# A state-space loop: the in-turn products go to the end of a step, and the sum of GpSimd's stack becomes an adding DMA

## The chip, the cores and the metric

The kernel runs on one core of one Trainium2 chip. The metric is the device time of one execution in microseconds (us), here the median of several runs. The engines go by these names: PE is TensorE (matrix products), DVE is VectorE, ACT is ScalarE, POOL is GpSimd, SP is the engine that issues most DMAs. Each engine works through its own queue in order and waits on semaphores for the others.

## The reference

Two layers work on 1024 latent tokens and 256 context tokens of width 1024. Layer 0 mixes the tokens by a diagonal state-space model (S5) in both directions, then comes a gated feed-forward layer; layer 1 is attention with a feed-forward layer. Only the S5 mixer is touched here. Cut to what matters:

```python
def s5_direction(u, h0, ar, ai, bbr, bbi, C_re, C_im, reverse, want_y):
    ug = u.reshape(Bn, L, S5_G, S5_GC).swapaxes(0, 1)
    br = jnp.einsum('lbgc,gpc->lbgp', ug, bbr)
    bi = jnp.einsum('lbgc,gpc->lbgp', ug, bbi)
    ...
    _, _, hr, hi = lax.associative_scan(s5_combine, (a_r, a_i, br, bi), reverse=reverse, axis=0)
    ...
    y = (jnp.einsum('lbgp,gcp->blgc', hr, C_re.astype(jnp.float32))
         - jnp.einsum('lbgp,gcp->blgc', hi, C_im.astype(jnp.float32))).reshape(Bn, L, D)
```

There are 64 groups of 16 channels, 64 complex states for each group, and two directions.

## The kernel before

The token axis is cut into blocks of 8 tokens, so that one scan runs over 160 block states. Each complex state is turned by a table of cosines and sines, so that the scan itself is real: a turn in, a scan with a real decay, a turn back. Two groups in both directions make one step of a loop, 32 steps of work in all (n = 0 to 32, with a drain). The engines' queues in this loop hold exactly the order in which the code is written (the line with `pinned.update`). What a step n does, by the names in the code:

- `stack_in(n+4)` makes the input matrices of a later step: two products on GpSimd, `sb` and `su`, and their sum into `sb`. `stack_out(n+6)` makes output matrices in the same manner on VectorE, `sc` and `su`; their sum is an adding DMA, issued from GpSimd. Sums that are owed stand in the list `owed`, and `settle` issues them.
- `turned(n+3)` transposes `sb` on TensorE into PSUM, ScalarE copies it to `bt`, and small products of `sc` with `bb1` build a lag kernel in PSUM. In even steps `lag_out` takes that to the tile `kt`, by two copies on ScalarE and one instruction on VectorE; a DMA stores it, and `lag_in` loads it as `mt`.
- `in_products(n+2)` multiplies `bt` with the tokens `ug` into two PSUM tiles `psA`, of which there are two in all. `in_turn(n+2)` multiplies these with the tables `tcs` and `tsn` to `ww` and `pq` on VectorE, and an adding DMA from GpSimd sums them into `ww`.
- `scans(n)` runs six scans from `ww` into `zz`, with the decay `r8` in PSUM. `turn_back(n)` makes `qc` and `qs` from `zz`, and `out_products(n-1)` multiplies those of the step before, and `ug` with `mt`, into an output tile that `out_copy` takes away on ScalarE.
- `tables_a`, `tables_b`, `tables_c` make the tables of step n+3: a part on ScalarE (`ty`, `tn`), one instruction on VectorE (`ty` from `tn`), and the sines on ScalarE.
- Every fourth step `load_u` loads the next `ug` into one of two buffers and ScalarE copies one column of it.

VectorE's queue of one step was: scans, `ww`, `pq`, `qc`, `qs`, `ty`, in even steps `kt`, then `sc`, `su`. All profile rows bear line 198, that of the helper which records each instruction, so the tiles' names tell them apart.

Of the kernel before, what the change touches and what calls it, by code (L numbers as in the profile page):

```python
# [18 lines left out]
F32 = mybir.dt.float32  # L19
# [164 lines left out]
def trunk(tc, I, out, dbg=None):  # L184
# [20 lines left out]
    V, S, Q, T, D_ = (Engine(*e) for e in zip("VSQTD", (nc.vector, nc.scalar, nc.gpsimd, nc.tensor, nc.sync)))  # L205
    dma = D_.dma_start

    def mul(o, a, b, e=V):
        e.tensor_tensor(o, a, b, op=ALU.mult)

    def add(o, a, b, e=V):
        e.tensor_tensor(o, a, b, op=ALU.add)
# [10 lines left out]
    def gather(o, a):  # L223

        Q.dma_start(o, a, accum_op=ALU.add)
# [14 lines left out]
    def pool(name, bufs=1, side="left", space=None):  # L240
        kw = {} if space is None else {"space": space}
        cm = tc.tile_pool(name=name, bufs=bufs, side=side, reuse_waits="tile", **kw)
        p = cm.__enter__()
        opened.append((p, cm))
        return p
# [461 lines left out]
    def w_in_norm(p, xc):  # L707

        acc = p.tile([128, 640], F32, name="acc", tag="nacc", bufs=1)
        square(acc, xc[:, 0])  # L710
        for f in range(1, 8):
            sq = p.tile([128, 640], F32, name="sq", tag="ns", bufs=3)
            square(sq, xc[:, f])
            add(acc, acc, sq, (V, Q)[f % 2])
        yield
        r = rstd_of(acc, D, 640, 2, psA)
        for f in range(8):
            mul(xc[:, f], xc[:, f], r, (V, Q)[f % 2])
        yield
# [31 lines left out]
    g = w_in_norm(st, x)  # L751
# [9 lines left out]
    g = w_in_norm(st, x)  # L761
# [18 lines left out]
    ge = pool("ge", 1, "right")  # L780
# [3 lines left out]
    def load_c(q):  # L784
        c = ge.tile([128, 2, 8, C16], F32, name="cc", bufs=6)
        dma(c.rearrange("p a b c -> p a (b c)"), I["c12"][q])
        coef[q] = c

    def sign_c(q):
        c = coef[q]  # L790
        S.activation(c[:, 0], c[:, 0], AF.Copy, scale=sg[:, 1:2])

    sh = [128, 4, TB, C16]
    AHEAD = 6

    owed = []

    def settle():

        for o, a in owed:  # L800
            gather(o, a)
        owed.clear()

    def stack(k, name, p_, x1, x2, e, p, nb):

        k0 = 4 * k

        def pw(t):
            return t.rearrange("p t g -> p g t")[:, k0:k0 + 4, :, None].to_broadcast(sh)

        def cf(t):
            return t[:, :, None, :].to_broadcast(sh)

        u = ge.tile(sh, F32, name="su", tag="su" + name, bufs=1 if e is Q else 2)
        a = p.tile(sh, F32, name=name, tag=name, bufs=nb)
        mul(a, pw(p_[0]), cf(x1), e)
        mul(u, pw(p_[1]), cf(x2), e)
        if e is Q:
            add(a, a, u, e)
        else:  # L820
            owed.append((a.rearrange("p g t c -> p (g t c)"), u.rearrange("p g t c -> p (g t c)")))
        return a.rearrange("p g t c -> p g (t c)")

    def stack_in(k):

        k0 = 4 * k
        sbs[k] = stack(k, "sb", bp, bb1[:, k0:k0 + 4], bb2[:, k0:k0 + 4], Q, ge, 2)
# [6 lines left out]
    def swap(k):  # L834

        cs = scs[k][0]
        cw = gp.tile([128, 4, 128], F32, name="cw", bufs=4)
        dma(cw[0:64], cs[64:128])
        dma(cw[64:128], cs[0:64])
        cws[k] = cw  # L840
# [40 lines left out]
    def lag_in(q):  # L881
        mt = gp.tile([128, 4, 128], F32, name="mt", bufs=3)
        for t in range(TB):
            dma(mt[16 * t:16 * t + 16],
                ktd[q][:, 0:16, 16 * (7 - t):16 * (7 - t) + 128].rearrange("g c k -> c g k"))
        mts[q] = mt

    def load_u(ft):
        ug = gp.tile([128, 8, JX], F32, name="ug")
        dma(ug[:, :, :J], ubd[ft].rearrange("t c g j -> (t c) g j"))  # L890
        copy(ug[:, :, J:JX], ug[:, :, 0:1])
        return ug
# [11 lines left out]
    def turns_in(t):  # L904

        return pairs(t)
# [4 lines left out]
    def tables_a(n):  # L911

        def flat(t):
            return t[:, :2 * sht[2]].rearrange("p (a b) -> p a b", a=2)[:, :, :2 * JX]

        ty = flat(wp.tile([128, 1024], F32, name="ty", tag="wr"))
        tn = flat(wp.tile([128, 1024], F32, name="tn", tag="wb", bufs=6))
        for i in range(4):
            l = slice((i % 2) * JX, (i % 2) * JX + JX)
            S.activation(ty[:, i // 2, l], idx[:, l], AF.Copy, scale=f8[:, 4 * n + i:4 * n + i + 1])  # L920
        S.activation(tn, ty, AF.Identity, bias=magic)
        tys[n] = ty, tn
# [50 lines left out]
    def in_products(n):  # L973

        bt, ug = bts.pop(n), ugs[n // 4]
        va = []
        for sw in range(2):
            v = psA()
            for i in range(4):
                d = i % 2  # L980
                T.matmul(v[:, i // 2, d * J:d * J + J], bt[:, i, 64 * sw:64 * sw + 128],
                         ug[:, (2 * n + i // 2) % 8, d:d + J], start=True, stop=True)
            va.append(v)
        return va

    def in_turn(n, va):

        pq = []
        for v, t, nm in zip(va, tab[n], ("ww", "pq")):
            p_ = gt.tile(sh4, F32, name=nm, tag=nm, bufs=NW if nm == "ww" else NPC)  # L990
            mul(p_.rearrange("p (g d) j -> p g d j", g=2),
                v[:, :, :2 * J].rearrange("p g (d j) -> p g d j", d=2), turns_in(t))
            pq.append(p_)
        owed.append(tuple(p_.rearrange("p a j -> p (a j)") for p_ in pq))
        return pq[0]

    def states(w):
        z = wp.tile([128, 1024], F32, name="zz", tag="wb", bufs=6)[:, :4 * J].rearrange("p (a b) -> p a b", a=4)
        Q.memset(z[:, 0::2, 0:1], 0.0)
        Q.memset(z[:, 1::2, JC - 1:JC], 0.0)  # L1000
        return w, z

    def scans(n, w, z):

        def scan(o, x_, i, init):
            m_ = o.shape[-1]
            V.tensor_tensor_scan(o, r8[:, 4 * n + i:4 * n + i + 1].to_broadcast([128, m_]), x_,
                                 init, op0=ALU.mult, op1=ALU.add)

        for i in (1, 3):  # L1010
            scan(z[:, i, 0:JC - 1][:, ::-1], w[:, i, 0:JC - 1][:, ::-1], i, 0.0)
        for i in (0, 2):
            scan(z[:, i, 1:J], w[:, i, 0:J - 1], i, 0.0)
        for i in (1, 3):
            scan(z[:, i, JC:J][:, ::-1], w[:, i, JC:J][:, ::-1], i, z[:, i, 0:1])
# [35 lines left out]
    NS5 = 32  # L1051
    pend = {}
# [5 lines left out]
    for n in range(NS5 + 1):  # L1058
        if n % 4 == 0 and n + 4 < NS5:
            ugs[n // 4 + 1] = load_u(n // 4 + 1)  # L1060
        if n % 2 == 0 and (n + AHEAD + 2) // 2 < NS5 // 2:
            load_c((n + AHEAD + 2) // 2)
        if n + 2 < NS5:
            swap(n + 2)
        if n % 2 == 1 and (n + 1) // 2 < NS5 // 2:
            lag_in((n + 1) // 2)
        if n + 4 < NS5:
            stack_in(n + 4)
        settle()
        if n + 2 < NS5:  # L1070
            va = in_products(n + 2)
        if n < NS5:
            scans(n, *pend[n])
        if n + 3 < NS5:
            tables_a(n + 3)
        if n > 0:
            py = out_products(n - 1, rot)
        if n + 2 < NS5:
            pend[n + 2] = states(in_turn(n + 2, va))
            settle()  # L1080
        if n > 0:
            out_copy(n - 1, py)
        if n < NS5:
            rot = turn_back(n, pend.pop(n)[1])
        if n + 3 < NS5:
            tables_b(n + 3)
        if n + 3 < NS5:
            turned(n + 3)
            if n % 2 == 0:
                lag_out((n + 2) // 2)  # L1090
        if n + AHEAD < NS5:
            stack_out(n + AHEAD)
        if n % 2 == 1 and (n + AHEAD + 1) // 2 < NS5 // 2:
            sign_c((n + AHEAD + 1) // 2)
        if n + 3 < NS5:
            tables_c(n + 3)
        if n % 4 == 1 and n > 1:
            store_y(n // 4 - 1)
        if n == 28:
            ws = Weights([((I[a][i],), 8) for _ in range(2) for a, i in  # L1100
                          [("swg", i) for m in range(8) for i in (8 + m, m)] + [("swo", m) for m in range(8)]], 4, 2)
            ws.load()
        if n == 31:
            ws.ahead = 0
            ws.ahead = 0
            first_w = [ws.whole(8)]
# [43 lines left out]
    def tB():  # L1150
        return hB.tile([128, 2, 640], F32R, name="hb", tag="hb")
# [37 lines left out]
    for c in range(2):  # L1189
        av = []  # L1190
        for m in range(8):
# [10 lines left out]
            o = tB()  # L1202
# [610 lines left out]
    pend = []  # L1813
# [108 lines left out]
```

## Time and profile before

| | |
|---|---|
| time, median of 3 runs | 3428.85 us (3422.14 to 3429.99) |
| time of the profiled execution | 3414.58 us |
| its span, first to last instruction | 3412.8 us |
| TensorE (PE) busy | 3179.5 us, 93% |
| VectorE (DVE) busy | 2784.1 us, 82% |
| ScalarE (ACT) busy | 1745.9 us, 51% |
| GpSimd (POOL) busy | 1052.3 us, 31% |
| mean granted TensorE clock | 0.980 of full speed |

The shares are means over stages with different limits. The loop that is changed lies between about 204 us and 485 us of the span. Clock 1.00 is 2.4 GHz, 0.50 is 1.2 GHz. A row of the timeline gives the start, the duration, the engine, the operation with its written and read tiles, and in brackets how long the engine was idle before it and what ended that.

### The profile page before, as it was taken

What the parts mean: (1) busy time and instruction counts of PE and PEld (TensorE: products, weight loads), DVE (VectorE), ACT (ScalarE), POOL (GpSimd) and SP (SyncE); (2) the same over time, 40 slices, a digit from 0 to 9 for tenths busy, and PEclk for the clock granted to TensorE, in tenths of its full rate; (3) what the DMA queues carried; (4) which work ended last, traced back from release to release, by engine and by line L of the source; (5) the groups of instructions that cost most, each with busy time, mean ns of one, the idle gap of its engine ahead of it and who ended that gap; (6) DMA issues with size and microseconds to landing.
All of it is one profiled execution on the core that took longest, in us unless ns stands there. A gap on an engine that the chain in (4) does not pass through costs nothing. (4 is left out here: it accounts for less than half of the span.)

```text
span 3412.8 us, 55310 instructions
## 1 busy us (share of the span) xinstructions
PE 3179.5 (93%) x20468; PEld 2922.0 (86%) x20468; DVE 2784.1 (82%) x4640; ACT 1745.9 (51%) x3234; POOL 1052.3 (31%) x812
## 2 busy tenths in 40 slices
PE   5887789999999999999999989989989899999999
PEld 3877779999999999999988767767777799889998
DVE  5979977878888989888866678888886788898887
ACT  4456662425333444344555557777775544454443
POOL 2356620101112121121234345555554411221111
PEclk7989989999999999999999999999999999999999
DMA  6457776552333323322335742222225333233232
GB/s 231 131 128 157 154 184 212 207 184 88 106 108 101 120 87 112 114 72 83 123 118 159 198 138 76 81 74 75 72 72 162 126 103 105 90 124 105 97 109 75
DMA packets 191775, 414.69 MB, mean 122 GB/s; under 512 B 22224, under 2 KB 73360, under 8 KB 190480
## 3 DMA queue, kind: packets, MB, share of 16 engines
q1 hardware_dynamic: 182288, 392.27, 36.0%
q0 software_dynamic: 9216, 18.88, 3.1%
q8 instruction: 162, 2.65, 0.3%
q14 instruction: 109, 0.89, 0.1%
HBM read 326.89 MB, written 53.49 MB: 111 GB/s over the span
## 5 line engine op out<-in xcount | busy, mean ns | idle before, releaser
L198 PE MATMUL psB<-hs,wb 128*128 128x320 f32 (+1 forms) x7392 | 1002.2, 297 | 24.4 <-DVE wb L198 16.9
L198 PEld LDWEIGHTS psB<-hs,wb 128*128 128x128 f32 x7392 | 991.1, 189 | 34.3 <-DVE wb L198 22.1
L198 ACT ACTIVATE wb<-wr 128x512 fp32r<-128x512 f32 (+3 forms) x704 | 404.7, 593 | 431.2 <-PE psB L198 219.6
L198 DVE TENSOR_TENSOR wb<-wr,wb 128x512 fp32r<-128x512 f32 (+3 forms) x704 | 492.3, 709 | 160.4 <-ACT wb L198 159.5
L198 PE MATMUL psB<-hb,wb 128*128 128x320 f32 (+1 forms) x3360 | 601.4, 340 | 10.5 <-ACT hb L198 4.7
L198 PEld LDWEIGHTS psB<-hb,wb 128*128 128x128 f32 x3360 | 544.8, 188 | 62.9 <-ACT hb L198 5.9
L198 POOL TENSOR_TENSOR ws<-wr 128x512 f32<-128x512 f32 x176 | 243.6, 1389 | 1151.1 <-DMA wr<-in_fi 535.4
L198 ACT ACTIVATE wb<-ws 128x512 fp32r<-128x512 f32 x352 | 218.9, 627 | 268.3 <-PE psB L198 191.9
L198 POOL TENSOR_TENSOR pl<-pf,ph 128x512 fp32r<-128x512 f32 x192 | 250.4, 1304 | 261.6 <-DVE ph L198 256.3
L198 DVE TENSOR_TENSOR wb<-ws,wb 128x512 fp32r<-128x512 f32 x352 | 273.2, 780 | 29.8 <-ACT wb L198 28.0
L198 PE MATMUL psA<-ha,wb 128*128 128x320 f32 x1680 | 250.2, 311 | 4.4 <-ACT ha L198 4.4
L198 PEld LDWEIGHTS psA<-ha,wb 128*128 128x128 f32 x1680 | 249.2, 190 | 5.0 <-ACT ha L198 4.6
L198 PE MATMUL psS<-kt,qt 128*128 128x512 f32 x768 | 213.1, 403 | 1.2 <-ACT p L198 1.1
L198 PEld LDWEIGHTS psT<-ident,p 128*128 128x128 f32 x1280 | 147.7, 140 | 72.4 <-issue 20.2
L198 PE MATMUL psT<-ident,p 128*128 128x128 f32 x1280 | 190.1, 275 | 20.2 <-DVE pl L198 17.3
L198 DVE TENSOR_REDUCE mx<-psS 128x1 f32<-128x1024 f32 x128 | 155.5, 1215 | 19.6 <-PE psS L198 19.0
L198 PEld LDWEIGHTS psS<-kt,qt 128*128 128x128 f32 x768 | 139.9, 189 | 29.0 <-ACT p L198 2.2
L198 POOL TENSOR_TENSOR acc<-acc,sq 128x640 f32<-128x640 f32 (+1 forms) x51 | 82.1, 1610 | 241.7 <-ACT sq L198 228.8
L198 ACT ACTIVATE p<-psS,mx,scq 128x1024 f32<-128x1024 f32 x128 | 153.9, 1202 | 0.0
L198 ACT ACTIVATE hb<-sg 128x640 fp32r<-128x640 f32 (+1 forms) x104 | 72.1, 693 | 152.9 <-DVE sg L198 152.6
L198 PE MATMUL psA<-ug,bt 128*128 128x160 f32 x512 | 94.1, 346 | 51.7 <-ACT bt L198 51.7
L198 PE MATMUL psO<-ph,vt 128*128 128x512 f32 x320 | 139.6, 436 | 2.4 <-DVE ph L198 0.4
(340 smaller groups left out, 5578.6 us busy)
## 6 DMA issues: line engine op xcount, KB each, us to landing
wr<-in_fi SPq DMA_DIRECT2D x176, 512.0 KB
wr<-in_mt SPq DMA_DIRECT2D x80, 512.0 KB
wr<-in_swg SPq DMA_DIRECT2D x32, 512.0 KB
wr<-in_fo SPq DMA_DIRECT2D x64, 256.0 KB
wr<-in_fo SPq DMA_DIRECT2D x32, 384.0 KB
ww<-pq POOLq DMA_DIRECT2D x32, 320.0 KB, 4.1
kdr<-big SPq DMA_DIRECT2D x32, 320.0 KB
kt<-kdr SPq DMA_DIRECT2D x16, 640.0 KB
```

The lines of the kernel that those rows point to most:

```text
L198: r = f(*a, **k)
```

## The change

The in-turn products of step n+2 (`ww`, `pq`) go from the middle of VectorE's step to its end. `stack_in(n+4)` goes from the head of the step to behind them, so that its two GpSimd products stand behind the issue of `ww`'s DMA. The third GpSimd instruction, the sum, is replaced by an adding DMA that is issued behind `sc`'s. The scratch tile `su` of GpSimd's stack has two buffers instead of one. `settle(n)` issues only the first n owed sums.

```diff
-    def settle():
-
-        for o, a in owed:
+    def settle(n=None):
+
+        for o, a in owed[:n]:
             gather(o, a)
-        owed.clear()
+        del owed[:n]
...
-        u = ge.tile(sh, F32, name="su", tag="su" + name, bufs=1 if e is Q else 2)
+        u = ge.tile(sh, F32, name="su", tag="su" + name, bufs=2)
         a = p.tile(sh, F32, name=name, tag=name, bufs=nb)
         mul(a, pw(p_[0]), cf(x1), e)
         mul(u, pw(p_[1]), cf(x2), e)
-        if e is Q:
-            add(a, a, u, e)
-        else:
-            owed.append((a.rearrange("p g t c -> p (g t c)"), u.rearrange("p g t c -> p (g t c)")))
+        owed.append((a.rearrange("p g t c -> p (g t c)"), u.rearrange("p g t c -> p (g t c)")))
...
-        if n + 4 < NS5:
-            stack_in(n + 4)
-        settle()
         if n + 2 < NS5:
             va = in_products(n + 2)
...
-        if n + 2 < NS5:
-            pend[n + 2] = states(in_turn(n + 2, va))
-            settle()
...
         if n % 2 == 1 and (n + AHEAD + 1) // 2 < NS5 // 2:
             sign_c((n + AHEAD + 1) // 2)
+        if n + 2 < NS5:
+            pend[n + 2] = states(in_turn(n + 2, va))
+            owed.insert(0, owed.pop())
+            settle(1)
+        if n + 4 < NS5:
+            stack_in(n + 4)
+        settle()
```

On GpSimd, one step in the middle of the loop, before:

```order
L198 DMA ww_2655<-pq_2657 128x640
L198 TENSOR_TENSOR sb_2711<-bpr_128,bb1_132 128x512
L198 TENSOR_TENSOR su_2710<-bpi_129,bb2_133 128x512
L198 TENSOR_TENSOR sb_2711<-sb_2711,su_2710 128x512
L198 DMA sc_2688<-su_2687 128x512
```

and now (the numbers of tiles differ between the two programs):

```order
L198 DMA ww_2679<-pq_2681 128x640
L198 TENSOR_TENSOR sb_2688<-bpr_128,bb1_132 128x512
L198 TENSOR_TENSOR su_2687<-bpi_129,bb2_133 128x512
L198 DMA sc_2675<-su_2674 128x512
L198 DMA sb_2688<-su_2687 128x512
```

The sum of `sb` and `su`, third among the computing instructions before, is now a DMA, the last of the step. On VectorE, an even step before, from the end of `in_turn` of one step to that of the next:

```order
L198 TENSOR_TENSOR pq_2752<-psA_2721,tsn_2693 128x640
L198 TENSOR_TENSOR qc_2759<-zz_2563,tcs_2506 128x640
L198 TENSOR_TENSOR qs_2760<-zz_2563,tsn_2507 128x640
L198 SCALAR_TENSOR_TENSOR ty_2732<-tn_2733,ty_2732 128x2x322
L198 SCALAR_TENSOR_TENSOR kt_2780<-dmask_1072,dk_1074,psB_2670 128x16
L198 TENSOR_TENSOR sc_2786<-cpr_130,cc_2514 128x512
L198 TENSOR_TENSOR su_2785<-cpi_131,cc_2514 128x512
L198 SCALAR_TENSOR_TENSOR zz_2659<-r8_126,ww_2655 128x31 x2
L198 SCALAR_TENSOR_TENSOR zz_2659<-r8_126,ww_2655 128x159 x2
L198 SCALAR_TENSOR_TENSOR zz_2659<-r8_126,zz_2659,ww_2655 128x128 x2
L198 TENSOR_TENSOR ww_2846<-psA_2812,tcs_2789 128x640
L198 TENSOR_TENSOR pq_2848<-psA_2817,tsn_2790 128x640
```

and now:

```order
L198 TENSOR_TENSOR pq_2681<-psA_2621,tsn_2600 128x640
L198 SCALAR_TENSOR_TENSOR zz_2589<-r8_126,ww_2585 128x31 x2
L198 SCALAR_TENSOR_TENSOR zz_2589<-r8_126,ww_2585 128x159 x2
L198 SCALAR_TENSOR_TENSOR zz_2589<-r8_126,zz_2589,ww_2585 128x128 x2
L198 TENSOR_TENSOR qc_2746<-zz_2589,tcs_2507 128x640
L198 TENSOR_TENSOR qs_2747<-zz_2589,tsn_2508 128x640
L198 SCALAR_TENSOR_TENSOR ty_2727<-tn_2728,ty_2727 128x2x322
L198 SCALAR_TENSOR_TENSOR kt_2767<-dmask_1072,dk_1074,psB_2657 128x16
L198 TENSOR_TENSOR sc_2773<-cpr_130,cc_2515 128x512
L198 TENSOR_TENSOR su_2772<-cpi_131,cc_2515 128x512
L198 TENSOR_TENSOR ww_2776<-psA_2711,tcs_2693 128x640
L198 TENSOR_TENSOR pq_2778<-psA_2716,tsn_2694 128x640
```

`pq` was followed by `qc`; now the scans of the next step follow it. On TensorE the order is as before. These rows stand there in the same even step, and `kt_2767` reads what they write to `psB_2657`; `sb_2688` is the stack whose products GpSimd begins behind `pq_2681`:

```order
L198 MATMUL psB_2751<-ident_64,sb_2688 128x128 x4
L198 MATMUL psB_2657<-sc_2489,bb1_132 32x112 x2
L198 MATMUL psB_2657<-cc_2139,bb1_132 32x16 x2
L198 MATMUL psB_2657<-sc_2489,bb1_132 32x112 x2
L198 MATMUL psB_2657<-cc_2139,bb1_132 32x16 x2
```

Nothing moved among these five; what feeds them did.

## Rows read from the trace of the kernel before

**Rows 1.** Busy time by stretch: length, PE, PEld, DVE, ACT, POOL, clock, DMA share, GB/s.

```profile
212.00:478.00 266.00, 207.14 (x1606) 198.80 (x1605) 260.54 (x398) 166.15 (x359) 163.73 (x192) 0.92 0.72 152
```

**Rows 2.** VectorE's groups from 203 to 478 us: busy, mean ns, idle before.

```profile
L198 DVE TENSOR_TENSOR qs<-zz,tsn 128x640 f32<-128x640 f32 x31 | 58.6, 1890 | 0.0
L198 DVE SCALAR_TENSOR_TENSOR ty<-tn,ty 128x644 f32<-128x644 f32 x29 | 52.6, 1813 | 0.0
L198 DVE TENSOR_TENSOR ww<-psA,tcs 128x640 f32<-128x640 f32 x30 | 23.9, 795 | 0.7 <-ACT tcs L198 0.5
```

**Rows 3.** Timeline, VectorE and GpSimd, part of a step.

```profile
308.43 0.79 DVE L198 TENSOR_TENSOR ww<-psA,tcs 128x640 f32<-128x640 f32 x1
...
309.14 0.81 DVE L198 TENSOR_TENSOR pq<-psA,tsn 128x640 f32<-128x640 f32 x1
...
310.25 0.85 POOL L198 DMA_DIRECT2D ww<-pq  x1 [2.18 <-DVE pq L198]
310.61 3.37 DVE L198 TENSOR_TENSOR qs<-zz,tsn 128x640 f32<-128x640 f32 x1
310.81 1.43 POOL L198 TENSOR_TENSOR sb<-bpr,bb 128x512 f32<-128x512 f32 x1
311.87 1.41 POOL L198 TENSOR_TENSOR su<-bpi,bb 128x512 f32<-128x512 f32 x1
```

**Rows 4.** Timeline of VectorE, `pq` of four steps (0, 9, 10, 28).

```profile
206.61 0.81 DVE L198 TENSOR_TENSOR pq<-psA,tsn 128x640 f32<-128x640 f32 x1
...
292.20 0.81 DVE L198 TENSOR_TENSOR pq<-psA,tsn 128x640 f32<-128x640 f32 x1
...
298.81 0.81 DVE L198 TENSOR_TENSOR pq<-psA,tsn 128x640 f32<-128x640 f32 x1
...
461.90 0.81 DVE L198 TENSOR_TENSOR pq<-psA,tsn 128x640 f32<-128x640 f32 x1
```

**Rows 5.** Two GpSimd DMAs, landing of the second; all `sc` DMAs, median to landing.

```profile
299.75 0.86 POOL L198 DMA_DIRECT2D sc<-su  x1
...
300.41 1.16 POOL L198 DMA_DIRECT2D ww<-pq  x1
...
DMA to landing us min/median/max: 6.0/6.0/6.0
...
sc<-su POOLq DMA_DIRECT2D x32, 256.0 KB, 4.2
```

**Rows 6.** Timeline, from `turned` to `kt` and through the next `in_products`.

```profile
450.97 0.60 PE L198 MATMUL psB<-ident,sb 128*128 128x128 f32 x4
...
452.52 2.44 PE L198 MATMUL psA<-ug,bt 128*128 128x160 f32 x16
452.63 0.42 ACT L198 ACTIVATE kt<-psB 128x112 f32<-128x112 f32 x2 [0.15 <-PE psB L198]
...
453.08 0.23 DVE L198 SCALAR_TENSOR_TENSOR kt<-dmask,dk,psB 128x16 f32<-128x16 f32 x1 [0.82 <-ACT kt L198]
...
456.16 0.43 PE L198 MATMUL psB<-ug,mt 128*128 128x160 f32 x2
```

**Rows 7.** Timeline of VectorE, from `kt` to the scans.

```profile
213.22 0.22 DVE L198 SCALAR_TENSOR_TENSOR kt<-dmask,dk,psB 128x16 f32<-128x16 f32 x1
...
214.56 1.08 DVE L198 TENSOR_TENSOR_SCAN zz<-r,ww 128x31 f32<-128x31 f32 x4
```

**Rows 8.** Timeline, the load of `ug` and ScalarE behind it.

```profile
277.37 0.44 PE L198 MATMUL psB<-ug,mt 128*128 128x160 f32 x2
...
277.84 0.57 SPq L198 DMA_DIRECT2D ug<-ub  x1
...
282.97 0.22 ACT L198 ACTIVATE ug<-ug 128x8 f32<-128x8 f32 x1 [2.54 <-DMA ug<-ub]
...
286.35 0.43 ACT L198 ACTIVATE kt<-psB 128x112 f32<-128x112 f32 x2
```

**Rows 9.** Timeline of TensorE, `in_products` behind a long wait.

```profile
206.84 4.63 PE L198 MATMUL psA<-ug,bt 128*128 128x160 f32 x16 [4.82 <-ACT bt L198]
```

## The prediction, made before the changed kernel ran

> **What bounds the kernel now.** I read the stretch table first, since the change touches one stage. In the state-space loop VectorE (DVE) is busy 260.54 of 266 us and TensorE (PE) 207.14 [rows 1]: the loop runs at VectorE's pace. Next the groups of VectorE's work in the loop: `qs` and `ty` take 1890 and 1813 ns in the mean, though `ww` and `pq`, as large, take about 0.8 us [rows 2, 3]. The timeline says why: a `qs` that normally ends in about 0.8 us takes 3.37 when GpSimd's products `sb` and `su` begin 0.2 us behind it, and ends 0.70 us behind the second product [rows 3]. `ww` and `pq`, which read PSUM, keep their length. The marks of `pq` give the pace: 28 steps (0 to 28) in 461.90 - 206.61 = 255.3 us, 9.1 a step, while the step from 292.20 to 298.81, in which GpSimd's work lay beside PSUM readers, took 6.61 [rows 4]. About 2.5 us a step is thus lost to GpSimd, and this is what the change can get at.
>
> **The change part by part.** Time in a step is counted from the end of the `pq` before it.
>
> *Products beside the scans.* GpSimd issues `ww`'s DMA 0.30 us behind `pq`, begins `sb` 0.56 later and `su` 1.06 after that; with 1.41 for `su` the products end at 3.33 [rows 3]. The scans, which read `r8` in PSUM, need about 1.8 us (6.61 less 1.45 for `ww` and `pq`, 1.2 for `sc` and `su`, 2.2 for three of 0.73; estimated from [rows 3, 4, 7]). Then `qc` comes at 1.7, is held to 3.33 and ends at 4.0 instead of 2.5: 1.5 us lost. The add on GpSimd, which held `ty` or `sc`, is gone. A step held by VectorE alone is 6.6 + 1.5 = **8.1 us**.
>
> The Trainium skill, page "SBUF — State Buffer", section "SBUF: two separate sides", says that a VectorE instruction with two SBUF inputs and a GpSimd instruction that reads SBUF lock each other out of a shared port pair, whole instructions at a time. The stretched `qs` beside the unstretched `ww` agrees. By that rule alone this change is a gain; that result is the first rival below.
>
> *The sum by DMA.* The stack of step n+4 is now multiplied at the end of step n, and its sum is a DMA behind the products and behind `sc`'s DMA. Of two GpSimd DMAs in a row the second began 0.66 behind the first [rows 5]: it is issued at 3.33 + 0.66 = 4.0. Landing: 4.2 us is the median of `sc`'s DMAs, mostly alone; 6.0 that of a 320 KB one 0.66 behind another [rows 5]. The new one is of the second kind but 256 KB: I take 5.3. So the sum is there at a = **9.3 us** into step n+1; bounds 8.2 (4.2) and 10.0 (6.0).
>
> The Trainium skill, page "DMA: Bandwidth & Descriptors", section "Anatomy of one DMA — SWDGE (gpsimd) path", fits such a DMA with 2.0 us plus bytes over 436 GB/s, an estimate of 2.6 us for 256 KB. The median of 4.2 here is well over that; with 2.6 the fourteen waits below would be some 38 us shorter in all.
>
> *Who waits for it.* In even steps `lag_out` needs the transposes and small products of `turned(n+3)`, and VectorE's `kt` stands in its queue ahead of `sc`, `su`, `ww`, `pq`. From the first transpose to `kt` on VectorE took 453.08 - 450.97 = 2.1 us, through TensorE and ScalarE [rows 6]; from `kt` to the end of `pq` it is 1.34 to the end of `sc` and `su` [rows 7], 0.71 and 0.81 [rows 3], 2.9 in all. Without the wait `kt` would come at about 5.5; it comes at 9.3 + 2.1 = 11.4, and an even step takes 11.4 + 2.9 = **14.3 us**. The held `qc` is hidden there. In odd steps no VectorE instruction needs that step's transposes: 8.1 stands.
>
> *Every fourth step* (n = 4, 8 ... 24) `load_u` reuses the buffer that `out_products(n-1)` reads, and ScalarE copies a column of `ug` ahead of everything else of its step. Before, TensorE ran `in_products(n+2)` early, since `in_turn(n+1)` gave PSUM back in mid-step. Now PSUM is free only as the step begins, and the odd step's transposes start at 9.3 - 8.1 = 1.2 of it. `in_products` follow 1.55 later, at 2.75; the second product with `mt` 3.64 after that, at 6.4 [rows 6]; `ug`'s DMA 0.47 behind it, at 6.9; ScalarE gets `ug` 5.13 later, at 12.0, and its `kt` copies end 3.81 after that, at 15.8 [rows 8]. With 2.9 such a step takes **18.7 us**.
>
> *TensorE after long waits.* It will wait about 5 us in odd steps. After a wait of 4.82 us the same 16 matmuls took 4.63 us, after none 2.44 [rows 9, 6]; the granted clock of the loop is 0.92 in the mean [rows 1], so part of it ran at the lower of the two levels already. In six `ug` steps this is on the path: 6 x 2.2 = 13 us; in eight other even steps it pushes the transposes back by about 0.6 (`out_products` end at 9.9 instead of before 9.3, an estimate): 5 us. **18 us**, from 0 to 31 (2.2 in all fourteen).
>
> *At nothing:* the stack sums ahead of the loop (TensorE has the input projection's products to do meanwhile; without that cover, one or two landings, some 5 to 10 us), the second `su` buffer, and the ends: in step 0 `pq` moves back by 3.6 us, and behind the last `pq` 2.4 less is left. The new transfers (32 of 256 KB) meet DMA engines at a share of 0.72 [rows 1]; that is in the bounds of the landing.
>
> *Sum for steps 1 to 28:* 6 x 18.7 + 8 x 14.3 + 14 x 8.1 = 340.0; steps 26 to 28 lack `sc` and `su`, 3 x 1.2 = 3.6 less: 336.4. Against 255.3 that is +81, and with TensorE's 18, **+99 us**. Nothing later takes it back: the stage behind reads what this loop writes. The profiled execution took 3414.6 us (span 3412.8), 14.3 under the median of the runs; 3513.6 there, and **3528 us** against the median of 3428.85.
>
> **The rivals.**
> 1. *Faster: the sum lands before it is missed.* Then all steps are 8.1 (even ones 8.2): 28 x 8.15 - 3.6 = 225, or -31: 3398 us. For it: the loop is paced by VectorE today, and the held time is real. Against: it decides where a + 2.1 is at most `kt`'s free time of 5.5, so a up to 3.4, and the products alone end at 3.33. Chance 0.03. No change (within 0.3%) needs all even steps at about 10.4, thus a landing within 1.4 us, a third of the median in [rows 5]: 0.02.
> 2. *The chain holds, but with TensorE at full speed* (a = 8.2 to 9.3): +66 to +81, 3495 to 3510. For it: the waits that I expect in even steps are about 2 us, less than half of the one in [rows 9]. Against: those of odd steps are as long as that one. Chance 0.24.
> 3. *`ug` is not late:* if its buffer came free otherwise, these steps are like other even ones, 6 x 4.4 = 26 less than +81: +55, 3484. Against: its DMA is issued 0.47 us behind that very product [rows 8]. Chance 0.08.
> 4. *Landings get worse:* the loop's accumulating DMAs go from two to three a step. With a at 10.0 and TensorE slow in all even steps: 14 x 0.7 + 31 + 81 = +122, 3551, and more if they pass 6 us. Chance 0.08.
>
> **How the numbers follow.** The forecast (+81 to +122, likeliest +99) has 0.55. The range leaves out rivals 1 and 4's far end and a little of 3: 3478 to 3556, which is +49 to +127. A difference under 0.3%, 10 us, could not be told from none. Faster 0.03, same 0.02, slower 0.95.
>
> **What would show it.** VectorE no longer 98% busy in the loop; its idle time ahead of `kt`, ended by ScalarE's `kt`, some 5 to 6 us in even steps; the first transpose waiting for the DMA `sb<-su`; steps alternating between about 8 and 14 with one near 19 to 21 in four; ScalarE waiting some 4 us or more for `ug`; `qs` and `ty` at about 0.8 us with `qc` at about 2.3 in odd steps; the loop some 100 us longer and all later stages as before. I am wrong if `kt` does not wait, or if the transposes find `sb` there already.

## The result, and the profile of the changed kernel

The changed kernel takes 3514.06 us in the median of 4 runs (3512.39 to 3521.41), the kernel before 3425.49 in runs beside it (4 runs, 3418.33 to 3429.99): ratio 1.0265, 95% interval 1.024 to 1.029, slower by 88.6 us. The profiled execution of the changed kernel is that of 3512.39 us, span 3510.6; its span is 97.8 longer than the one of before.

Where the time went is told by the marks of `pq`, as in [rows 4]. Timeline of VectorE in the changed kernel, `pq` of steps 0 and 28:

```profile
206.11 0.81 DVE L198 TENSOR_TENSOR pq<-psA,tsn 128x640 f32<-128x640 f32 x1
...
553.19 0.81 DVE L198 TENSOR_TENSOR pq<-psA,tsn 128x640 f32<-128x640 f32 x1
```

Steps 1 to 28 take 553.19 - 206.11 = 347.1 us, against 255.3 in [rows 4]: +91.8. With step 0 (0.5 earlier) and step 29 (4.88 instead of 7.10) the last `pq` stands at 558.07 instead of 469.00: +89.1, close to the difference of the medians. The other 8.7 of the spans lie behind the loop. In the fourteen profiles of this study that part took 2942.8 to 2959.1 us with no order by what the loop does, and the two executions stood differently to their medians: that of before 10.9 under it, this one 1.7. I don't count them to the change.

The same stretch as in [rows 1], and VectorE's groups from 203 to 570 us, which answer to [rows 2]:

```profile
212.00:478.00 266.00, 174.13 (x1171) 164.60 (x1170) 173.24 (x284) 121.90 (x267) 103.62 (x150) 0.80 0.66 135
```

```profile
L198 DVE TENSOR_TENSOR qc<-zz,tcs 128x640 f32<-128x640 f32 x31 | 64.0, 2064 | 3.7
...
L198 DVE TENSOR_TENSOR qs<-zz,tsn 128x640 f32<-128x640 f32 x32 | 26.0, 812 | 0.0
...
L198 DVE SCALAR_TENSOR_TENSOR ty<-tn,ty 128x644 f32<-128x644 f32 x29 | 23.9, 824 | 85.7 <-ACT tn L198 85.7
...
L198 DVE SCALAR_TENSOR_TENSOR kt<-dmask,dk,psB 128x16 f32<-128x16 f32 x15 | 3.5, 230 | 30.7 <-ACT kt L198 30.7
```

VectorE's own work became cheaper, as was meant: `qs` fell from 1890 ns to 812 and `ty` from 1813 to 824, while `qc` alone is held now, 2064. But VectorE is busy 173.24 of 266 us instead of 260.54, and what it waits for are two tiles of ScalarE. The waits from 203 to 570 us (total, times, longest) say who is behind that:

```profile
DVE ty L198 <- ACT tn L198: 85.7, 14, 11.0
...
PE psA L198 <- DVE ww L198: 67.5, 14, 8.7
...
ACT ug L198 <- DMA ug<-ub: 49.9, 6, 9.1
PE psB L198 <- DMA sb<-su: 48.1, 19, 4.4
...
DVE kt L198 <- ACT kt L198: 30.7, 14, 4.3
```

TensorE waits for the sum's DMA (`sb<-su`) 19 times and for PSUM, which `ww` gives back, 14 times; ScalarE waits for `ug` in six steps.

The steps show two kinds of long step. Timeline of the changed kernel, from step 11 to 14 (odd steps 11 and 13 take 8.19 us, step 12 takes 19.55, step 14 takes 15.62):

```profile
333.08 1.42 POOL L198 DMA_DIRECT2D sb<-su  x1
...
336.81 0.81 DVE L198 TENSOR_TENSOR pq<-psA,tsn 128x640 f32<-128x640 f32 x1
...
337.56 1.09 PE L198 MATMUL psB<-ident,sb 128*128 128x128 f32 x4 [3.58 <-DMA sb<-su]
...
340.40 2.68 PE L198 MATMUL psA<-ug,bt 128*128 128x160 f32 x16
...
344.29 0.44 PE L198 MATMUL psB<-ug,mt 128*128 128x160 f32 x2
...
344.75 0.57 SPq L198 DMA_DIRECT2D ug<-ub  x1
...
350.49 0.22 ACT L198 ACTIVATE ug<-ug 128x8 f32<-128x8 f32 x1 [8.58 <-DMA ug<-ub]
...
352.88 0.83 DVE L198 SCALAR_TENSOR_TENSOR ty<-tn,ty 128x644 f32<-128x644 f32 x1 [10.49 <-ACT tn L198]
...
354.27 0.23 DVE L198 SCALAR_TENSOR_TENSOR kt<-dmask,dk,psB 128x16 f32<-128x16 f32 x1 [0.56 <-ACT kt L198]
...
356.36 0.81 DVE L198 TENSOR_TENSOR pq<-psA,tsn 128x640 f32<-128x640 f32 x1
...
356.59 4.61 PE L198 MATMUL psA<-ug,bt 128*128 128x160 f32 x16 [8.69 <-DVE ww L198]
...
360.82 1.43 POOL L198 DMA_DIRECT2D sb<-su  x1
...
364.55 0.81 DVE L198 TENSOR_TENSOR pq<-psA,tsn 128x640 f32<-128x640 f32 x1
...
367.55 0.63 PE L198 MATMUL psB<-ident,sb 128*128 128x128 f32 x4 [3.48 <-DMA sb<-su]
...
369.00 1.42 POOL L198 DMA_DIRECT2D sb<-su  x1
...
369.85 3.31 PE L198 MATMUL psA<-ug,bt 128*128 128x160 f32 x16
...
373.68 0.83 DVE L198 SCALAR_TENSOR_TENSOR ty<-tn,ty 128x644 f32<-128x644 f32 x1 [3.56 <-ACT tn L198]
...
375.94 0.63 PE L198 MATMUL psB<-ident,sb 128*128 128x128 f32 x4
...
378.08 0.23 DVE L198 SCALAR_TENSOR_TENSOR kt<-dmask,dk,psB 128x16 f32<-128x16 f32 x1 [3.57 <-ACT kt L198]
...
380.17 0.81 DVE L198 TENSOR_TENSOR pq<-psA,tsn 128x640 f32<-128x640 f32 x1
```

Landing of the DMA issued at 369.00, the sum of step 14's own stack:

```profile
DMA to landing us min/median/max: 6.8/6.8/6.8
```

Read step 14, from the end of `pq` at 365.36. The transposes of the odd step before it had to wait until 367.55 for a sum issued at 360.82: 6.73 us. TensorE then does the small products, `in_products` (3.31) and `out_products`, and comes to this step's transposes at 375.94 with almost no idle time ahead of them. This step's own sum landed only just before, at 369.00 + 6.8 = 375.8: two chains end there together. `kt` follows 2.14 later and the end of `pq` 2.90 after that. In step 12 the chain through `ug` is the longer one: its DMA goes out 7.13 us into the step, ScalarE has it 5.74 later, and `ty`, `kt` and the rest of VectorE's queue stand behind it.

### The profile page after: what moved, and what is told of

Same layout as the page of the kernel before. It is cut to its first block, busy times and chain, and to the rows that moved or that the text cites. A ratio compares the mean times of both kernels' runs of the same rounds, so it can differ in the third digit from the quotient of the medians.

```text
span 3510.6 us, 55314 instructions
## 1 busy us (share of the span) xinstructions
PE 3212.9 (92%) x20468; PEld 2948.3 (84%) x20468; DVE 2757.1 (79%) x4640; ACT 1745.8 (50%) x3234; POOL 1016.5 (29%) x812
## 5 line engine op out<-in xcount | busy, mean ns | idle before, releaser
L198 PE MATMUL psA<-ug,bt 128*128 128x160 f32 x512 | 108.5, 383 | 76.0 <-DVE ww L198 67.5
L198 PEld LDWEIGHTS psA<-ug,bt 128*128 128x128 f32 x512 | 100.5, 256 | 77.7 <-ACT tcs L198 65.1
```

The lines of the kernel that those rows point to most:

```text
L198: r = f(*a, **k)
```

## The experiments

The theory on record had two parts: (1) in even steps `kt` waits for the landing of the stack's sum, which now starts in the same step; (2) every fourth step `ug` comes late, as its buffer is given back late. The rivals were traffic of the new DMAs, GpSimd's products, and TensorE's clock. Each kernel was timed beside runs of the kernel before (medians 3422.5 to 3424.5), and ratios are against it.

**The sum back on GpSimd, all else as changed (e1).**

```diff
-        owed.append((a.rearrange("p g t c -> p (g t c)"), u.rearrange("p g t c -> p (g t c)")))
+        if e is Q:
+            add(a, a, u, e)
+        else:
+            owed.append((a.rearrange("p g t c -> p (g t c)"), u.rearrange("p g t c -> p (g t c)")))
```

> The changed order, but the stack's sum is GpSimd's add again, not a DMA. Theory (VectorE's kt waits for the sum's landing; ug comes late every fourth step): the sum is there about 5.1 us behind pq instead of 9 to 10.6, so even steps fall from 15.6 to about 10.2, the odd ones grow from 8.2 to about 9.3 (the add holds qs), the ug steps fall from 19 to about 16.6. Sum for steps 1 to 28 about 308 us against 255 before: span about 3465, some 50 over before and 45 under the changed kernel. Rival (the loss is the third adding DMA's traffic): without it the time is at before, 3413, or under it.

Measured: 3467.74 us, ratio 1.0132 [1.0113, 1.015]. Odd steps 9.26, even 10.28, those with `ug` 14.8 to 16.1. About half of the loss is thus the DMA in the sum's place; odd steps are 1.07 longer than in the changed kernel, since the add on GpSimd holds `qs` too.

**The sum by DMA in the old order (e2).**

```diff
-        u = ge.tile(sh, F32, name="su", tag="su" + name, bufs=1 if e is Q else 2)
+        u = ge.tile(sh, F32, name="su", tag="su" + name, bufs=2)
...
-        if e is Q:
-            add(a, a, u, e)
-        else:
-            owed.append(...)
+        owed.append(...)
```

> The old order, with the stack's sum as an adding DMA (and the second su buffer): one part of the change alone. Theory: there the products start in mid-step and kt stands 12 us or more behind them, so the landing is not missed; the add no longer holds VectorE. Steps of about 8.4 instead of 9.1: span about 3393, 20 under before. Rival (traffic of the third adding DMA): slower than before by 50 us or more.

Measured: 3412.73 us, ratio 0.9973 [0.9957, 0.9989]: a gain of about 10, less than expected. Here the adding DMAs of 256 KB cost less than they save, and the 50 us or more of the rival are not there: their traffic alone is not the cause of the loss. VectorE's groups in the loop:

```profile
L198 DVE TENSOR_TENSOR qs<-zz,tsn 128x640 f32<-128x640 f32 x32 | 44.2, 1380 | 0.0
```

`qs` falls only from 1890 to 1380: the products still lie beside it in part of the steps. One step takes 17.52 us, where `ty` waits 9.7 for ScalarE, which waits for `ug`.

**The stack one step earlier (e3)** (changed kernel, the products of step n+5 at the end of step n).

```diff
-        if n + 4 < NS5:
-            stack_in(n + 4)
+        if n + 5 < NS5:
+            stack_in(n + 5)
```

> The changed kernel, with the input stack made one step earlier (step n+5 instead of n+4, one more ahead of the loop), same DMAs. Theory: kt finds its transposes done, even steps fall from 15.6 to about 8.3; the ug steps stay late, about 16.6. Sum for steps 1 to 28 about 278: span about 3437, 25 over before. Rival (traffic, or the order of VectorE's work by itself): no change from the changed kernel, 3510.

Measured: 3457.42 us, ratio 1.0096 [1.0077, 1.0116]. 56.6 of the 88.6 are gone, so part (1) is shown; but some 74 were expected (a span of 3437 after 3510.6). Even steps without `ug` take 9.4 to 10.7 up to step 22, not 8.3. Timeline of such a step:

```profile
293.16 4.49 PE L198 MATMUL psA<-ug,bt 128*128 128x160 f32 x16 [9.66 <-DVE ww L198]
...
301.12 0.81 DVE L198 TENSOR_TENSOR pq<-psA,tsn 128x640 f32<-128x640 f32 x1
...
301.76 2.45 PE L198 MATMUL psA<-ug,bt 128*128 128x160 f32 x16
...
306.76 0.60 PE L198 MATMUL psB<-ident,sb 128*128 128x128 f32 x4
...
308.88 0.23 DVE L198 SCALAR_TENSOR_TENSOR kt<-dmask,dk,psB 128x16 f32<-128x16 f32 x1 [1.43 <-ACT kt L198]
```

The sum is there, and `kt` still waits, for TensorE. `in_products` can't start before `ww` and `pq` have given PSUM back: in the odd step before they waited 9.66 us for `ww` and took 4.49, so that the even step's begin at 301.76, right behind that step's transposes, and its own transposes at 306.76, behind `out_products`. That is a cost of `in_turn` standing last. The 9.66 us are long because the step before is one with `ug`; but in e5 below, where no step is held so long, even steps up to 26 still take 9.3 us or more, with the sums landed.

**A third buffer for `ug` (e4)** (changed kernel; room from `mt`, 3 to 2 buffers, and `cc`, 6 to 4).

```diff
-        ug = gp.tile([128, 8, JX], F32, name="ug")
+        ug = gp.tile([128, 8, JX], F32, name="ug", bufs=3)
```

> The changed kernel, with a third buffer for ug (room for it by two mt and four cc buffers instead of three and six), so that the load need not wait for out_products. Theory: the six ug steps fall from about 19 to that of the other even steps, 15.6; ScalarE's 50 us of waiting for ug go. Span about 3490, 20 under the changed kernel. Rival (ug's wait lies beside the wait for the stack): within 5 us of the changed kernel, 3510.

Measured: 3497.05 us, ratio 1.0222 [1.0203, 1.0242]: 17.0 less, as expected. The steps with `ug` take 15.4 to 18.2 instead of 18.3 to 20.1, near the other even ones (13.6 to 17.0).

**Both together (e5).**

> The changed kernel with both remedies: the input stack a step earlier and a third buffer for ug. Theory (these two waits are the whole loss): the six ug steps fall from about 16.5, as with the early stack alone, to the 9.4 to 10.7 of its other even steps, 38 us off its span of 3456: about 3418, near before (3413). Rival (something else in the new order costs too, such as the held qc or the PSUM that comes free late): 3435 or more.

Measured: 3418.74 us, ratio 0.9987 [0.9972, 1.0001], no difference from before: 95.3 of the changed kernel are back, more than 56.6 + 17.0, since in each edit alone the other wait still set some steps. Odd steps take 8.2 us, even ones 9.3 to 12.0 up to step 26.

**`lag_out` behind `in_turn` (e7)** (changed kernel), so that `kt` no longer stands ahead of `ww` and `pq` in VectorE's queue.

```diff
             turned(n + 3)
-            if n % 2 == 0:
-                lag_out((n + 2) // 2)
...
             settle(1)
+        if n + 3 < NS5 and n % 2 == 0:
+            lag_out((n + 2) // 2)
```

> The changed kernel with lag_out, and so VectorE's kt, behind the in-turn products instead of ahead of sc. Theory (kt holds up what stands behind it on VectorE): in even steps ww and pq no longer wait for kt; kt comes at 12.7 and the next scans right behind it, so even steps take about 12.9 instead of 15.6, and the ug steps about 1.4 less: 30 us off, span about 3480. Rival (ScalarE's tables, for which ty waits, set the step, and kt's wait lies beside it): no change, 3510.

Measured: 3482.85 us, ratio 1.0172 [1.0153, 1.019]. The place of `kt` in the queue is on the path; moved, part of its wait goes into the step behind (even steps without `ug` 9.2 to 10.8, some odd ones up to 11.6).

**The sum's DMA ahead of `sc`'s (e8)** (changed kernel).

```diff
             stack_in(n + 4)
+        owed.reverse()
         settle()
```

> The changed kernel, with the stack's adding DMA issued ahead of sc's instead of 0.66 us behind it. Theory (the time a at which the sum lands sets the even steps, and part of it is that the DMA comes second in the queue): a falls by 0.7 us of issue and up to 1.2 of landing, in 14 even steps: 10 to 27 us less, span about 3492. Rival (the landing is long because of the traffic of all queues, whoever goes first): 10 us less or none.

Measured: 3490.07 us, ratio 1.0188 [1.0163, 1.0213]: 24 less. Landing of the DMA `sb<-su`, in the changed kernel and, in the second fence, here:

```profile
DMA to landing us min/median/max: 3.2/4.9/6.9
```

```profile
DMA to landing us min/median/max: 3.2/3.7/5.4
```

The issue, expected 0.7 earlier, stayed at 3.65 us behind `pq`; the landing gained 1.2 in the median and 1.5 at the top, and the even steps without `ug` 1.1 to 3.4 up to step 26.

**Which version gains?** The next two (e10, and e11 with the third buffer for `ug`) take the old order, with the sum by DMA, and put the products behind the issue of `sc`'s DMA, beside the scans and `ww`, `pq`, which read PSUM.

```diff
+        settle()
         if n + 4 < NS5:
             stack_in(n + 4)
-        settle()
```

> The old order on VectorE with the sum by DMA, and on GpSimd the issue of sc's DMA, which waits for VectorE's su, ahead of the two products, so that the products run beside scans, ww and pq. Theory (GpSimd's products hold VectorE only where it works from SBUF alone): qs falls from 1380 ns in the mean, as with the old GpSimd order, to about 820; steps of about 7.3, every fourth longer by a wait for ug. Span about 3380. Rival (with three adding DMAs a step the DMA engines set the pace): no better than the sum by DMA in the old order, 3407.

> The same with a third buffer for ug. Theory: no step waits for ug any more, 28 steps of about 7.2 make 202 us against 255 before: span about 3362. Rival (the DMA engines, or TensorE with about 6.5 us of work a step, set the pace at 8 or more): 3390 or more.

Measured: 3426.0 (ratio 1.0006 [0.9996, 1.0016]) and 3425.03 (1.0004 [0.999, 1.0019]); both miss by some 45 to 60 us. The expected steps are there, 6.0 to 7.9 us in 22 of 28, but the six with `ug` take 14.6 to 19.4, with three buffers too. Timeline of the second, steps around `ug`:

```profile
263.84 5.65 SPq L198 DMA_DIRECT2D mt<-kd  x8
...
269.53 0.57 SPq L198 DMA_DIRECT2D ug<-ub  x1
...
277.46 0.22 ACT L198 ACTIVATE ug<-ug 128x8 f32<-128x8 f32 x1 [12.81 <-DMA ug<-ub]
...
279.91 0.83 DVE L198 SCALAR_TENSOR_TENSOR ty<-tn,ty 128x644 f32<-128x644 f32 x1 [11.52 <-ACT tn L198]
```

It is not the buffer here: `ug`'s DMA stands behind eight others in SP's queue (`lag_in`), ScalarE has its data 7.9 us after its issue, and ScalarE's copy of a column of `ug` is first in its step. So three kernels with this copy a step later: e10 with it (f1), e2 with it (f2) and the kernel before with it alone (f3).

```diff
-        copy(ug[:, :, J:JX], ug[:, :, 0:1])
         return ug
+    def wrap_u(ug):
+        copy(ug[:, :, J:JX], ug[:, :, 0:1])
...
             tables_c(n + 3)
+        if n % 4 == 1 and n + 3 < NS5:
+            wrap_u(ugs[n // 4 + 1])
```

> Sum by DMA, products behind sc's DMA, in_turn in its old place (e10), and ScalarE's copy of a column of ug moved from behind its DMA's issue to the end of the step after. In e10 22 of the 28 steps take 6.0 to 7.9 us and six take 14.7 to 19.4; in those ScalarE waits 69.8 us for ug's DMA and VectorE 62.0 for ScalarE's tn. Theory (the miss of e10 is this one copy: its work is held up in six steps and nothing else): these six steps fall to about 8, 6 x 10 = 60 us less: span about 3365, ratio 0.983. Rival (ug comes too late for its products too, so the wait only moves to TensorE's in_products two steps on): span over 3400.

> The kernel before with the sum by DMA (e2) and ScalarE's copy of ug's column a step later. In e2 ScalarE waits 30.8 us for ug and VectorE 20.2 for tn, of which one step of 17.5 us has most. Theory: 10 to 15 us less than e2: span about 3394. If the order of GpSimd's work decides the rest, f1 stays about 30 us ahead of this one.

> The kernel before with the late copy alone. There ScalarE waits 25.5 us for ug, but the steps that hold these waits take 10.4 us beside 10.25 for their neighbours: VectorE, held by GpSimd, hides them. Theory: 0 to 5 us less, span about 3410, so that the copy is worth something only where GpSimd no longer sets the pace. Rival (the copy is a cost by itself): 15 to 25 us less.

The first: 3393.32 us, ratio 0.9909 [0.9887, 0.993], the fastest here and 121 under the changed kernel, but its span of 3395.3 is 30 over the expectation. Its stretch of 212 to 478 us, and TensorE in one of the steps that are still long:

```profile
212.00:478.00 266.00, 226.78 (x1746) 216.74 (x1746) 207.22 (x406) 186.90 (x385) 129.38 (x189) 0.94 0.94 204
```

```profile
333.34 0.57 SPq L198 DMA_DIRECT2D ug<-ub  x1
...
343.67 0.51 PE L198 MATMUL psA<-ug,bt 128*128 128x160 f32 x2 [3.01 <-DMA ug<-ub]
...
346.71 4.10 PE L198 MATMUL psA<-ug,bt 128*128 128x160 f32 x14 [2.53 <-ACT ug L198]
```

The rival was right in part: in the longest case, with the DMA engines at a share of 0.94, `ug` lands 10.3 us after its issue, and the wait moves to `in_products`. How far the DMA engines themselves hold this kernel up, no run here shows.

The second: 3425.9 us, ratio 1.0008 [0.9994, 1.0023], 13 worse than without the late copy. It differs from the first only in the order of GpSimd's work, and is 33 us behind it, as its expectation had it. `qs` took 1876 ns in its mean from 203 to 470 us; in the first, from 203 to 440 us:

```profile
L198 DVE TENSOR_TENSOR qs<-zz,tsn 128x640 f32<-128x640 f32 x30 | 24.4, 814 | 0.0
```

The third: 3455.28, ratio 1.0095 [1.0065, 1.0125], where 0 to 5 us less were expected. Neither shows the gain that was expected of the late copy. Timeline of the third:

```profile
223.53 0.20 ACT L198 ACTIVATE ug<-ug 128x8 f32<-128x8 f32 x1
...
223.78 1.44 PE L198 MATMUL psA<-ug,bt 128*128 128x160 f32 x4 [6.63 <-ACT ug L198]
```

In the old order `in_products` run a step early, so the copy, now behind ScalarE's tables (which wait for a held `ty`), is missed at once. Where TensorE works ahead, the copy belongs early; that it hurts so much at 0.82 of the clock, against 0.92 before, I did not take apart.

## Why the prediction was right, and where it was off

- **Odd steps, 8.1:** 8.19. The products begin 0.86 behind `pq` and hold `qc` alone. The Trainium skill, page "SBUF — State Buffer", section "SBUF: two separate sides", has a VectorE instruction with two SBUF inputs and a GpSimd instruction that reads SBUF lock each other out of a shared port pair; the trace agrees, in `qs` at 812 ns away from the products and `qc` at 2064 beside them.
- **The step of 6.61 in [rows 4], misread:** GpSimd's work did not lie beside PSUM readers alone. `sb` began beside `qs`, `ty`, `sc` and `su`, and there GpSimd was the one held: its product took 3.08 us where others take 1.43 [rows 3], and VectorE lost nothing. The base of 6.6 us stands. From the timeline of the kernel before:

```profile
294.31 3.08 POOL L198 TENSOR_TENSOR sb<-bpr,bb 128x512 f32<-128x512 f32 x1 [0.15 <-PE psB L198]
294.40 0.81 DVE L198 SCALAR_TENSOR_TENSOR ty<-tn,ty 128x644 f32<-128x644 f32 x1
```

- **The sum at a = 9.3:** issue at 3.65 (4.0). The landing took 4.3 to 5.0 in most steps (5.3), but 6.2 to 6.9 in the odd steps in which `store_y` issues eight stores (5, 9, ... 25) and in most of the even steps behind them. So a is 8.0 to 8.6, or 9.8 to 10.8; the single value lies between the two. That the stores are the reason is a guess from the steps where it happens; no run moves them. The Trainium skill, page "DMA: Bandwidth & Descriptors", section "Anatomy of one DMA — SWDGE (gpsimd) path", gives 2.6 us as an estimate by its fit; the shortest landing here was 3.2 and the median 4.9, so the measurement decides.
- **Even steps, 14.3, or 14.9 with TensorE's 0.6:** 15.0 to 16.5 from step 6 to 26, 13.2 and 11.1 at the ends. From the transposes to `kt` it is 2.1 and on to `pq`'s end 2.9, as forecast. I had the even step's own sum end the wait at 9.3, and TensorE's queue 0.6 behind it. In steps 6 and 14 the two end within 0.1 us of each other, both late (transposes at 10.0 and 10.6). In steps 10, 18, 22 and 26 it is TensorE's queue (10.6 to 11.5), 0.3 to 2.7 us behind what the own sum alone would give. That queue is late because the odd step's sum before it is: its transposes start at 1.8 to 2.5, not 1.2, and `in_products` take up to 4.15.
- **Steps with `ug`, 18.7:** in step 12 `in_products` start at 2.78 (2.75), the second product with `mt` at 6.67 (6.4), the DMA goes at 7.13 (6.9), ScalarE has `ug` at 12.87 (12.0), and VectorE's `kt` comes at 16.65 (15.8). The chain is right, and the third buffer and the earlier stack confirm it. That the times agree so well is luck in part: the odd step's transposes began at -0.06, not 1.2, as its sum landed 8.0 us into the odd step, and the small products up to `in_products` then took 2.84 us at a granted clock of 0.50, where I had 1.55. In steps 8, 20 and 24 `in_products` start at 1.55 and the DMA goes at 5.66; in 4 and 16 it goes at 7.75 and 8.63.
- **TensorE after long waits, 18:** mis-sized, and in the wrong steps. The 4.61 us products behind a wait of 8.69 (granted clock 0.50) are in odd steps, where nobody waits. In the `ug` steps `in_products` took 4.1 and 4.2 us in two (4 and 16) and 2.4 to 2.7 in four, some 4 us too much in all where I had 13. In the eight other even steps they took 2.4 to 4.15, some 7 in all where I had 5. The six steps took 114.4 us in all where 112.2 + 13 were forecast; the eight other even ones 118.6 where 117.0 were (14.3 each, less 2.4 for missing `sc` and `su`, and 5), the odd ones 114.1 for 112.2. Sum 347.1 for 354.4.
- **Not foreseen:** `ty` waits too, 3.56 us in step 14, as ScalarE's `bt` copies wait for the same late sum. It costs nothing there, since `kt` comes later still. But the idle time that I put ahead of `kt`, 5 to 6 us, is thus split: 2.0 to 4.3 ahead of `kt` and 1.8 to 3.8 ahead of `ty` in the even steps without `ug`.
- **Rivals:** that the sum lands in time fell, by the waits for `sb<-su`; that `ug` is not late fell, by its third buffer; landings as long as in the fourth rival came in 11 of 28 steps; TensorE at full speed came true in three of the six steps with `ug`.

The forecast of +99 thus had the loop's two waits right and the term for TensorE some 9 too high in the steps with `ug`; the terms that were off partly cancel. The measured +88.6 lies inside the range.

## What to carry to other kernels

Taking an engine's contention away did not pay here, because the sum then started its trip through a DMA in the step that needs it: work out how late the consumer may be served (here, by the forecast's estimate, 3.4 us into the step, when the products alone had just ended) before work is put there. Where two late inputs meet in one step, neither edit alone shows its worth (56.6 and 17.0 alone, 95.3 together). The gain of 0.9% was in the order, with the products beside instructions that read PSUM and the sum landed before TensorE came to it, and it appeared only when the next wait, a small copy at the head of ScalarE's step, was moved as well.

## What was unexpected of the hardware

The load of `ug` reached the engine that waited for it 4.8 to 6.3 us after its issue in the changed kernel (DMA share 0.66 from 212 to 478 us), 5.3 to 7.9 in e11 (0.87) and 7.6 to 10.3 in three loads of f1 whose landing ended a wait (0.94). The kernel before has 4.7 to 6.2 at 0.72, so the share alone does not order them. An adding DMA of 256 KB landed 1.2 us earlier in the median when it was the first of a pair instead of 0.66 behind `sc`'s (3.7 for 4.9). The same sixteen products of the changed kernel took 2.41 us in step 10 (granted clock 1.00) and 4.60 in step 18 (0.50), each behind a wait of 2.80: the length of the last wait alone does not tell the clock.
